# Encoder layer on one core: the mixer's tiles laid out anew, and more products read in four passes over 16-byte granules

## Chip, core and metric

One core of a Trainium2 chip runs one launch of the kernel. The metric is the device time of the launch in microseconds (us), the median over runs. The profile shown is one further execution, taken by the hardware profiler.

## What is computed

One layer of a hybrid encoder over 512 positions of width 1024, all in float32:

```
x = x + 1/2 * SwiGLU_1(RMSNorm(x))               # d_ff 2752
h = RMSNorm(x); u = h @ w_in                     # fourier 512 | q 8x64 | k 2x64 | v 2x64
A = Re(DFT2 over (positions, group channels)) per group of 128 channels, then a linear map per group
B = GQA attention: RMSNorm of q and k per head, 2-D rotary, bidirectional softmax
x = x + concat([A, B]) @ w_out
x = x + 1/2 * SwiGLU_2(RMSNorm(x))
y = RMSNorm_final(x)
```

## The kernel before

Everything lies transposed: channels on the 128 partitions, the 512 positions along a partition, so a tile `[128, 512]` of float32 takes 2048 bytes of each partition. Every operand of a large product is split into a high part, rounded to the type float32r, and a low part, the rest, and a product of two numbers is three matmuls: high x high, high x low, low x high. The function `product` issues these three. TensorE (PE) holds a 128 x 128 stationary operand, the weights, loads the next one while it streams the moving operand past the current one (up to 512 columns), and adds into one of 8 PSUM banks.

`product` has two branches. With `turn=True` (line 182) the moving operand and the output are read and written through `turned`:

```
def turned(ap):
    return ap.rearrange("p (a b c) -> p b a c", b=4, c=4)
```

The 512 columns are taken as 32 x 4 granules of 4 numbers (16 bytes): first granule 0 of each group of four, in a second pass granule 1, and so on. The same numbers are multiplied in another order; the output is permuted alike, so the result lies where it lay. The other branch (lines 184, 186, 187) reads the columns straight through. Before the change the first-layer products, the gate and down products and the projections of q, k and v are turned.

Three stages follow each other: the first SwiGLU (`ffn`, with Strassen-like products of 256 columns in line 418), the mixer, and the second `ffn` with the end. In the mixer the order of the work on every engine is written out by hand in the string `ORDER`, whose words name operations: `s` + query tile, head, block is a score product (lines 1147 and 1148, two matmuls: moving `kst`, the keys, weights a block of `qa` or `qb`), `m` the row maximum on VectorE (line 1153, tile `mx`), `e` the exponential on ScalarE (line 1161), `t` the transposition of the probabilities on PE (line 1173), `h` and `l` the high part on ScalarE and the low part on VectorE (tiles `ph`, `pl`; the subtraction is the helper in line 126), `v` the product with the values (line 1216, two matmuls: moving `ph` and `pl`, weights `vst`). This runs over 4 query tiles, 2 key heads and 4 blocks. `d` are the Fourier transform's position products (line 1070, tiles `pos` and `both`, weights `eh`, `el`), `c` its channel products, `f` its projections (lines 1011 to 1013). `y0` to `y7` are the output projection: 8 tiles of 8 blocks, each a straight `product` whose moving operands are `mh`, `ml` (that is `eh` and `el` again, reused for the Fourier results) and `qa`, `qb` (reused for the attention's result). Operands wait for each other by semaphores; each engine works its own list in order.

The second `ffn` ends in `closing`: the last three output tiles are computed for the first half of the positions in the usual layout, and for the other half by tokens (`by_tokens`, line 532): the tokens' activations are the weights, and the moving operand `tw`, lying in the ring of weight slots, has 384 columns. Its two blocks of 128 tokens need 7 x 3 matmuls each; between them row factors are computed (lines 247 to 267, 1394, 1395) and the results are scaled and written (lines 1355, 1404, 1409, 1419).

Where a tile lies in a partition follows from the pools, in the order in which tiles are allocated; `room` allocates a few unused bytes, `FRONT`, `LOWER`, `NEAR` and `FURTHER` shift operands within a larger tile. In the turned products moving operands begin 16 bytes past a multiple of 128 and weights 64 bytes past one; scores, values, `both` and the output products have both at 64.

Of the kernel before, what the change touches and what calls it, by code (L numbers as in the profile page):

```python
# [7 lines left out]
F32R = mybir.dt.float32r  # L8
# [17 lines left out]
FURTHER_IN = "f0", "f1", "f2", "f3"  # L26
ROOM = 64
FRONT, LOWER, NEAR = 16, -12, 4
NS = 12

GROUPS1 = ((0, "t", 1, 2), range(3, 9), range(9, 15), range(15, 21))
# [53 lines left out]
def encoder(ctx, tc, A, out):  # L85
# [8 lines left out]
    def room(pool, n):  # L94


        pool.tile([P, n // 4], F32, name=f"room{len(rooms)}")
        rooms.append(n)
# [76 lines left out]
    def turned(ap):  # L175
        return ap.rearrange("p (a b c) -> p b a c", b=4, c=4)
# [103 lines left out]
    def ffn(norm, after, wgu, wd, wdt, groups, opening, closing):  # L280
# [6 lines left out]
        with tc.tile_pool(name=f"act{n_}", bufs=1) as ap, tc.tile_pool(name=f"sums{n_}", bufs=2) as sp:  # L287
# [7 lines left out]
            def place(j):  # L295
# [3 lines left out]
            own, shared = slots[:KD], slots[KD:]  # L299

            tw = [
                ring[:, 3 * i * KD * P : 3 * i * KD * P + PLACES * LAST * P]
                .rearrange("p (m c) -> p m c", c=LAST * P) for i in range(2)
            ]

# [214 lines left out]
            def by_tokens(ps, c, group):  # L520

                t = slice(c * P, (c + 1) * P)
                for i in range(LAST):
                    nc.tensor.matmul(
                        ps[:, i * P : (i + 1) * P], x[KD - LAST + i][:, t], ident, is_transpose=True,
                        start=i == 0, stop=False, skip_group_check=True,
                    )
                for j in group:
                    h, l = (at[:, where[j], o, t] for o in range(2))
                    whi, wlo = (w[:, j - group[0]] for w in tw)  # L530
                    for a, b in ((h, whi), (l, whi), (h, wlo)):
                        nc.tensor.matmul(
                            ps[:, : LAST * P], a, b, start=False, stop=j == group[-1] and b is wlo, skip_group_check=True
                        )
                    yield

# [207 lines left out]
    n2 = Norm(2)  # L744
    with tc.tile_pool(name="mix", bufs=1) as mp, tc.tile_pool(name="mixt", bufs=1) as mt:

        room(mp, 192)
        more_tile = mp.tile([P, 2 * KD * P + ROOM], F32R, name="more")
        more = [slot_at(more_tile, i) for i in range(2)]
        plain.extend(more)  # L750
# [4 lines left out]
        cos = mp.tile([P, S], F32, name="cos")  # L755
        sin = mp.tile([P, S], F32, name="sin")
        chan = mp.tile([P, 4, P], F32R, name="chan")
        both = mp.tile([P, S], F32R, name="both")
        pos = mp.tile([P, 4 * 258 + 3 * 256], F32R, name="pos")
        room(mp, 32)  # L760

        coss = [[pos[:, (2 * p + i) * 258 : (2 * p + i + 1) * 258] for i in range(2)] for p in range(2)]
        sins = [[None, pos[:, 1032:1288]], [pos[:, 1288:1544], pos[:, 1544:1800]]]
        sc = mp.tile([P, 4, 10], F32, name="sc")
        room(mp, 32)


        ops = {}
# [136 lines left out]
        def query_ops(t):  # L905
            name = f"q{t}"
            rope_ops(name, qkg[:, 0:1])

            @op(f"{name}.ah")
            def _():  # L910
                qa[t] = mp.tile([P, S], F32R, name=f"qa{t}")
                nc.scalar.copy(qa[t][0:HD], rots[name][0:HD])

            @op(f"{name}.al")
            def _():
                lows(qa[t][HD:P], rots[name][0:HD], qa[t][0:HD])

            @op(f"{name}.bh")
            def _():
                qb[t] = mp.tile([P, S], F32R, name=f"qb{t}")  # L920
                nc.scalar.copy(qb[t][HD:P], rots[name][HD:P])

            @op(f"{name}.bl")
            def _():
                lows(qb[t][0:HD], rots[name][HD:P], qb[t][HD:P])

        kw = tp.tile([P, 4, 2, HD], F32, tag="wide", bufs=1, name="kw")
        kst = [[mp.tile([P, S], F32R, name=f"ks{v}{o}") for o in range(2)] for v in range(2)]

        def key_ops():  # L930

# [22 lines left out]
                op(f"k{v}.2")(lambda own=own, oth=oth, h2=h2: nc.scalar.copy(h2[oth], rots["k"][own]))  # L954
                op(f"k{v}.3")(lambda own=own, h1=h1, h2=h2: lows(h2[own], rots["k"][own], h1[own]))

        vst = mp.tile([P, 2, 4, 2, HD], F32R, name="vst")

        @op("vt")
        def _():  # L960
# [26 lines left out]

        eh, el = ([[mp.tile([P, 2, 256], F32R, name=f"e{n}{h}{i}") for i in range(2)] for h in range(2)] for n in "hl")  # L990

        for i in range(4):
            weight_ops(f"f{i}", A["winf"][i].rearrange("p a (b c) -> p (a b) c", c=P))
# [66 lines left out]
        def position_ops(g):  # L1060


            gs = slice(g % 2 * P, (g % 2 + 1) * P)
            dh, dl = hh[2 + g % 2], hl[2 + g % 2]
            name = f"d{g}"

            def add(w, m, t):
                ps, first = banks[name], not started
                started.append(t)
                nc.tensor.matmul(  # L1070
                    ps[:, t], w, m, start=first, stop=len(started) == 12, skip_group_check=True
                )

            started = []

            def sums(o):
                if not started:
                    banks[name] = bank_for(name, 1)
                for i in range(2):
                    h, l = (e[g // 2][i][:, o, gs] for e in (eh, el))  # L1080
                    t, m = (slice(256, 512), sins) if o else (slice(0, 258), coss)
                    if o and i == 0:
                        add(h, both, slice(0, S))
                        add(l, both, slice(0, S))
                    else:
                        add(h, m[0][i], t)
                        add(l, m[0][i], t)
                    add(h, m[1][i], t)

            op(f"{name}0")(lambda: sums(0))  # L1090
            op(f"{name}1")(lambda: sums(1))
            op(f"{name}.h")(lambda: nc.scalar.copy(dh, banks[name]))

            @op(f"{name}.l")
            def _():
                lows(dl, banks[name], dh)
                read(name)
# [41 lines left out]
        def score_ops(t, b, c):  # L1139
            n = f"{t}{b}{c}"  # L1140
            f = sc[:, c, 2 + 2 * t + b : 3 + 2 * t + b]

            @op(f"s{n}")
            def _():
                q = (qa, qb)[b][t][:, c * P : (c + 1) * P]
                sps[n] = bank_for(f"s{n}")
                nc.tensor.matmul(sps[n], q, kst[b][0], start=True, stop=False)  # L1147
                nc.tensor.matmul(sps[n], q, kst[b][1], start=False, stop=True)  # L1148

            @op(f"m{n}")  # L1150
            def _():
                mxs[n] = mx = tp.tile([P, 1], F32, tag="mx", bufs=8, name=f"mx{n}")
                nc.vector.tensor_reduce(out=mx, in_=sps[n], axis=AX.X, op=ALU.max, negate=True)
                nc.vector.tensor_tensor(out=mx, in0=mx, in1=f, op=ALU.mult)

            @op(f"e{n}")
            def _():
                if t not in zs:
                    zs[t] = tp.tile([P, 4, 2], F32, tag="z", bufs=2, name=f"z{t}")
                prob[t, b, c] = temp(f"e{n}")  # L1160
                nc.scalar.activation(
                    prob[t, b, c], sps[n], AF.Exp, bias=mxs[n], scale=f, accum_out=zs[t][:, c, b : b + 1]
                )
                read(f"s{n}")
# [42 lines left out]
        def attended_ops(t, b, kc):  # L1207
            n = f"{t}{b}{kc}"

            @op(f"v{n}")  # L1210
            def _():
                if kc == 0:
                    outs[t, b] = bank_for(f"o{t}{b}")
                w = vst[:, b, kc].rearrange("p a e -> p (a e)")
                for i, p in enumerate(parts[n]):
                    nc.tensor.matmul(outs[t, b], w, p, start=kc == 0 and i == 0, stop=kc == 3 and i == 1)  # L1216

            if kc < 3:
                return
            own = slice(b * HD, (b + 1) * HD)  # L1220

            @op(f"o{t}{b}.c")
            def _():
                if t not in pair:
                    pair[t] = tp.tile([P, S], F32, tag="u", name=f"oo{t}")
                nc.scalar.copy(pair[t][own], outs[t, b][HD:P])

            @op(f"o{t}{b}.a")
# [14 lines left out]
        def output_ops(d):  # L1243
            weight_ops(f"o{d}", A["wo"][d])
            name = f"y{d}"

            def step(k):
                if k == 0:
                    banks[name] = bank_for(name)
                whi, wlo = ws[f"o{d}"]  # L1250
                m = (mh[k], ml[k]) if k < 4 else (qa[k - 4], qb[k - 4])
                product(banks[name], whi[:, k, :], wlo[:, k, :], *m, k == 0, k == KD - 1)

            for k in range(KD):
# [309 lines left out]
```

## Time and profile before

| | us |
|---|---|
| median of 3 runs | 829.09 |
| lowest and highest | 829.08, 829.82 |
| profiled execution, whole | 829.21 |
| profiled execution, span from the first to the last instruction | 827.4 |

A row of a timeline gives the start, the duration, the engine (PE matmul, PEld weight load, DVE VectorE, ACT ScalarE, POOL GpSimd), the line, the operation, output<-inputs, and in brackets how long the engine was idle before and who released it. Rows of the same operation that follow each other are merged, with their count (x). A row of the chain of waits has start, duration, engine, output and line. A row of the windows has, for each engine, its busy time and its number of instructions, then the granted TensorE clock (1.00 is full speed) and the DMA engines' share.

### The profile page before, as it was taken

How to read it: one execution, taken by the hardware profiler on the slowest of the kernel's cores; microseconds unless marked ns; L12 is line 12 of the kernel's file. 1: busy time of each engine (PE TensorE's matmuls, PEld its weight loads, DVE VectorE, ACT ScalarE, POOL GpSimd, SP SyncE). 2: the span in 40 equal slices, each digit the busy share in tenths (PEclk: the TensorE clock that was granted, in tenths of full speed). 3: DMA queues.
4: the chain of work that ended last, by engine and by line, in shares of the span. 5: the costliest groups of instructions: out<-in, count | busy, mean ns of one | idle time of the engine just before them, and what ended most of it. 6: DMA issues, size and time to landing. Idle time of an engine off the chain costs nothing.

```text
span 827.4 us, 13668 instructions
## 1 busy us (share of the span) xinstructions
PE 820.0 (99%) x5406; PEld 750.9 (91%) x5406; DVE 639.4 (77%) x1005; ACT 464.6 (56%) x778; POOL 30.7 (4%) x34
## 2 busy tenths in 40 slices
PE   9999999999999999999999999999999999999997
PEld 7889999899989998888998888899988999899986
DVE  7998896489757847799998388998955896479573
ACT  7764663167424744778786357556632673256462
POOL 0110000000000000221000000100000000000001
PEclk9999999999999999999999999999999999999999
DMA  7664322323243213622020224443232332322222
GB/s 256 180 144 172 122 90 77 122 103 140 78 139 107 71 46 110 205 82 65 26 77 27 83 87 124 115 166 122 90 121 95 131 112 65 135 103 96 69 76 103
DMA packets 31169, 89.58 MB, mean 108 GB/s; under 512 B 3713, under 2 KB 8833, under 8 KB 31105
## 3 DMA queue, kind: packets, MB, share of 16 engines
q1 hardware_dynamic: 27776, 82.61, 29.4%
q0 software_dynamic: 2608, 5.12, 3.3%
q10 hardware_dynamic: 720, 0.98, 0.3%
q8 instruction: 42, 0.69, 0.3%
q14 instruction: 23, 0.18, 0.1%
HBM read 84.24 MB, written 2.10 MB: 104 GB/s over the span
## 4 chain that ended last, share of the span: by engine, by line
PE 97%; issue 1%; DVE 1%; DMA 0%; ACT 0%; POOLq 0%; POOL 0%; DVEq 0%
PE dn L182 25%; PE r L418 23%; PE q L418 12%; PE gu L182 8%; PE p L418 6%; PE mix L182 4%; PE gu L706 3%; PE mix L187 2%; PE mix L186 2%; PE mix L184 2%; PE mix L1216 2%; PE mix L1173 2%; PE mix L1147 1%; PE mix L1013 1%; PE mix L1148 1%; PE mix L1011 1%
## 5 line engine op out<-in xcount | busy, mean ns | idle before, releaser
L418 PE MATMUL r<-rt,ring 128*128 128x256 f32 x1686 | 209.3, 276 | 0.0
L182 PE MATMUL dn<-at,ring 128*128 128x512 f32 x900 | 203.3, 380 | 0.4 <-DVE ring L126 0.4
L418 PEld LDWEIGHTS r<-rt,ring 128*128 128x128 f32 x1686 | 200.4, 188 | 0.8
L182 PEld LDWEIGHTS dn<-at,ring 128*128 128x128 f32 x900 | 168.0, 188 | 29.8 <-DVE ring L126 1.6
L418 PE MATMUL q<-rt,ring 128*128 128x256 f32 x840 | 106.6, 276 | 0.0
L126 DVE TENSOR_TENSOR ring<-s,ring 128x1024 fp32r<-128x1024 f32 x70 | 85.5, 1221 | 23.9 <-ACT ring L377 20.8
L418 PEld LDWEIGHTS q<-rt,ring 128*128 128x128 f32 x840 | 100.4, 188 | 0.0
L541 DVE SCALAR_TENSOR_TENSOR gx<-dn,gx 128x512 f32<-128x512 f32 x61 | 41.9, 688 | 67.5 <-PE dn L182 67.5
L377 ACT CAST ring<-s 128x1024 fp32r<-128x1024 f32 x70 | 73.5, 1050 | 28.0 <-PE p L418 13.7
L168 ACT CAST ring<-raw_dn 128x768 fp32r<-128x768 f32 (+3 forms) x58 | 45.2, 783 | 71.4 <-PE dn L182 62.3
L126 DVE TENSOR_TENSOR ring<-raw_dn,ring 128x768 fp32r<-128x768 f32 (+3 forms) x58 | 51.6, 892 | 5.6 <-PE r L418 4.4
L418 PE MATMUL p<-rt,ring 128*128 128x256 f32 x420 | 53.3, 276 | 0.0
L126 DVE TENSOR_TENSOR ring<-raw_g,ring 128x1024 fp32r<-128x1024 f32 x35 | 42.7, 1221 | 11.2 <-PE p L418 10.2
L418 PEld LDWEIGHTS p<-rt,ring 128*128 128x128 f32 x420 | 50.2, 188 | 0.0
L182 PE MATMUL gu<-ring 128*128 128x512 f32 x216 | 48.9, 381 | 0.0
L182 PEld LDWEIGHTS gu<-ring 128*128 128x128 f32 x216 | 40.4, 188 | 6.9
L377 ACT CAST ring<-raw_g 128x1024 fp32r<-128x1024 f32 x35 | 36.8, 1052 | 16.1 <-DMA raw_g<-in_wgu 8.9
L426 ACT COPY p<-r 128x256 f32<-128x256 f32 x35 | 12.9, 370 | 46.4 <-PE r L418 46.1
L450 ACT ACTIVATE g<-g 128x512 f32<-128x512 f32 x35 | 22.2, 633 | 23.6 <-DVE g L449 23.3
L386 ACT CAST ring<-raw_u 128x512 fp32r<-128x512 f32 x35 | 21.8, 624 | 16.6 <-PE q L418 15.9
L254 POOL TENSOR_TENSOR r<-ms,mhalf 128x4 f32<-128x4 f32 (+1 forms) x4 | 4.3, 1071 | 660.9 <-DVE ms L247 660.9
L463 DVE TENSOR_TENSOR u<-g,u 128x512 f32<-128x512 f32 x35 | 24.1, 687 | 6.1 <-ACT u L462 6.0
(300 smaller groups left out, 1362.0 us busy)
## 6 DMA issues: line engine op xcount, KB each, us to landing
raw_g<-in_wgu SPq DMA_DIRECT2D x35, 512.0 KB, 3.6
raw_u<-in_wgu SPq DMA_DIRECT2D x35, 512.0 KB, 4.4
raw_dn<-in_wd SPq DMA_DIRECT2D x40, 384.0 KB, 3.1
raw_gu<-in_wgu SPq DMA_DIRECT2D x12, 512.0 KB, 3.5
raw_o<-in_wo SPq DMA_DIRECT2D x8, 512.0 KB, 3.5
raw_dn<-in_wd SPq DMA_DIRECT2D x8, 448.0 KB, 3.3
raw_wq<-in_wins SPq DMA_DIRECT2D x4, 512.0 KB, 4.3
raw_f<-in_winf SPq DMA_DIRECT2D x4, 512.0 KB, 4.2
```

Source lines behind the costliest of these rows:

```text
L126: nc.vector.tensor_tensor(out=lo, in0=src, in1=asf(hi), op=ALU.subtract)
L168: nc.scalar.copy(hi[:, :n, :], raw[:, :n, :])
L182: nc.tensor.matmul(ps, a, b, start=first and b is mhi and a is whi, stop=last and a is wlo)
L184: nc.tensor.matmul(ps, whi, mhi, start=first, stop=False)
L186: nc.tensor.matmul(ps[:, t], whi, mlo[:, t], start=False, stop=False)
L377: nc.scalar.copy(hi, src)
L386: nc.scalar.copy(hi, src)
L418: nc.tensor.matmul(ps[:, t], a[:, ks], b[:, i, t], start=first and i == 0 and o == 0, stop=i == KH - 1 and o == 2, skip_group_check=not first,
L450: nc.scalar.activation(b["g"], b["g"], AF.Silu)
L463: nc.vector.tensor_tensor(out=u, in0=b["g"], in1=u, op=ALU.mult)
L541: nc.vector.scalar_tensor_tensor(out=x[d][:, t], in0=ps[:, t], scalar=0.5, in1=x[d][:, t], op0=ALU.mult, op1=ALU.add)
L706: nc.tensor.matmul(turned(pss[c]), w[:, k % 2, c], turned(m[k]), start=k == 0 and m is hh and w is hi, stop=k == KD - 1 and w is lo,)
```

## The change

Four families of products go through `turned` as well: the scores, the values, the position products with `both`, and the eight output products (by `turn=True`). So do the last 384-column products, whose moving operand `tw` also begins 160 bytes (`ASIDE`, 40 numbers) further on. In the mixer the tiles are laid out in another order: the keys `kst`, `both` and `pos` come first; `qa`, `qb`, `eh`, `el` and `vst` become slices of one tile `near`, shifted by `NEAR` (4 numbers, 16 bytes); then follow `more`, `cos`, `sin` and `chan`. Moving operands of the output products then begin 16 bytes past a multiple of 128 against weights at 64; those of scores, values, `both` and the last products at 96 against weights at 16. The tiles of the temporary pool `mixt` all move by 96 bytes. The instructions, their number and their order on every engine stay; a few waits are attached to other instructions, among them the exp table load (line 1161), which gets the wait for the `mx` that the first exponential needs.

```
-                ring[:, 3 * i * KD * P : 3 * i * KD * P + PLACES * LAST * P]
+                ring[:, 3 * i * KD * P + ASIDE : 3 * i * KD * P + ASIDE + PLACES * LAST * P]
...
-                            ps[:, : LAST * P], a, b, start=False, stop=j == group[-1] and b is wlo, skip_group_check=True
+                            turned(ps[:, : LAST * P]), a, turned(b), start=False, stop=j == group[-1] and b is wlo,
+                            skip_group_check=True,
...
-        room(mp, 192)
+        room(mp, 96)
+        kst = [[mp.tile([P, S], F32R, name=f"ks{v}{o}") for o in range(2)] for v in range(2)]
+        both = mp.tile([P, S], F32R, name="both")
+        pos = mp.tile([P, 4 * 258 + 3 * 256], F32R, name="pos")
+        near = mp.tile([P, 18 * S + 2 * NEAR], F32R, name="near")
+        part = [near[:, NEAR + i * S : NEAR + (i + 1) * S] for i in range(16)]
+        eh, el = ([[part[4 * n + 2 * h + i]... for i in range(2)] for h in range(2)] for n in range(2))
+        vst = near[:, NEAR + 16 * S : NEAR + 18 * S].rearrange("p (v c o e) -> p v c o e", v=2, c=4, o=2)
+        room(mp, 32)
         more_tile = mp.tile([P, 2 * KD * P + ROOM], F32R, name="more")
...
-        both = mp.tile([P, S], F32R, name="both")
-        pos = mp.tile([P, 4 * 258 + 3 * 256], F32R, name="pos")
...
-                qa[t] = mp.tile([P, S], F32R, name=f"qa{t}")
+                qa[t] = part[8 + t]
...
-                qb[t] = mp.tile([P, S], F32R, name=f"qb{t}")
+                qb[t] = part[12 + t]
...
-                        add(h, both, slice(0, S))
-                        add(l, both, slice(0, S))
+                        add(h, turned(both), slice(0, S), turned)
+                        add(l, turned(both), slice(0, S), turned)
...
-                nc.tensor.matmul(sps[n], q, kst[b][0], start=True, stop=False)
-                nc.tensor.matmul(sps[n], q, kst[b][1], start=False, stop=True)
+                nc.tensor.matmul(turned(sps[n]), q, turned(kst[b][0]), start=True, stop=False)
+                nc.tensor.matmul(turned(sps[n]), q, turned(kst[b][1]), start=False, stop=True)
...
-                    nc.tensor.matmul(outs[t, b], w, p, start=kc == 0 and i == 0, stop=kc == 3 and i == 1)
+                    nc.tensor.matmul(turned(outs[t, b]), w, turned(p), start=kc == 0 and i == 0, stop=kc == 3 and i == 1)
...
-                product(banks[name], whi[:, k, :], wlo[:, k, :], *m, k == 0, k == KD - 1)
+                product(banks[name], whi[:, k, :], wlo[:, k, :], *m, k == 0, k == KD - 1, turn=True)
```

More of the change, by code (lines that the diff above doesn't have):

```diff
@@ L28 @@
 FRONT, LOWER, NEAR = 16, -12, 4
+ASIDE = 40
 NS = 12
@@ L745, in encoder @@
     with tc.tile_pool(name="mix", bufs=1) as mp, tc.tile_pool(name="mixt", bufs=1) as mt:
-        room(mp, 192)
+        room(mp, 96)
[4 more added lines that the diff above has]
+        part = [near[:, NEAR + i * S : NEAR + (i + 1) * S] for i in range(16)]
+        eh, el = ([[part[4 * n + 2 * h + i].rearrange("p (a b) -> p a b", a=2) for i in range(2)] for h in range(2)] for n in range(2))
+        vst = near[:, NEAR + 16 * S : NEAR + 18 * S].rearrange("p (v c o e) -> p v c o e", v=2, c=4, o=2)
+        room(mp, 32)
         more_tile = mp.tile([P, 2 * KD * P + ROOM], F32R, name="more")
@@ L757, in encoder @@
         chan = mp.tile([P, 4, P], F32R, name="chan")
-        both = mp.tile([P, S], F32R, name="both")
-        pos = mp.tile([P, 4 * 258 + 3 * 256], F32R, name="pos")
-        room(mp, 32)
         coss = [[pos[:, (2 * p + i) * 258 : (2 * p + i + 1) * 258] for i in range(2)] for p in range(2)]
@@ L764, in encoder @@
         sc = mp.tile([P, 4, 10], F32, name="sc")
-        room(mp, 32)
         ops = {}
@@ L927, in encoder @@
         kw = tp.tile([P, 4, 2, HD], F32, tag="wide", bufs=1, name="kw")
-        kst = [[mp.tile([P, S], F32R, name=f"ks{v}{o}") for o in range(2)] for v in range(2)]
         def key_ops():
@@ L955, in key_ops @@
                 op(f"k{v}.3")(lambda own=own, h1=h1, h2=h2: lows(h2[own], rots["k"][own], h1[own]))
-        vst = mp.tile([P, 2, 4, 2, HD], F32R, name="vst")
         @op("vt")
@@ L985, in encoder @@
             value_ops(v)
-        eh, el = ([[mp.tile([P, 2, 256], F32R, name=f"e{n}{h}{i}") for i in range(2)] for h in range(2)] for n in "hl")
         for i in range(4):
@@ L1065, in position_ops, with add @@
             name = f"d{g}"
-            def add(w, m, t):
+            def add(w, m, t, order=lambda ps: ps):
                 ps, first = banks[name], not started
@@ L1070, in add @@
                 nc.tensor.matmul(
-                    ps[:, t], w, m, start=first, stop=len(started) == 12, skip_group_check=True
+                    order(ps[:, t]), w, m, start=first, stop=len(started) == 12, skip_group_check=True
                 )
```

## The prediction

> **What bounds the kernel now.** I read the page first (busy shares, chain), then the windows by stage, then the timeline of PE around each group of products that the change touches, and last who waits for whom.
>
> ```profile
> span 827.4 us, 13668 instructions
> PE 820.0 (99%) x5406; PEld 750.9 (91%) x5406; DVE 639.4 (77%) x1005; ACT 464.6 (56%) x778; POOL 30.7 (4%) x34
> PE 97%; issue 1%; DVE 1%; DMA 0%; ACT 0%; POOLq 0%; POOL 0%; DVEq 0%
> ...
> core 0: us, PE busy (x) PEld busy (x) DVE busy (x) ACT busy (x) POOL busy (x), PEclk, DMA share, GB/s
> 356.00:449.00 93.00, 92.98 (x615) 83.61 (x614) 87.51 (x179) 71.29 (x145) 8.73 (x7) 1.00 0.17 52
> 449.00:492.00 43.00, 43.00 (x196) 35.72 (x195) 26.18 (x37) 17.49 (x26) 0.00 (x0) 1.00 0.23 74
> 809.00:828.00 19.00, 12.45 (x86) 11.80 (x85) 7.11 (x17) 4.00 (x10) 3.23 (x5) 0.90 0.31 111
> ```
>
> TensorE is the chain: 97% of it, busy in 820.0 of 827.4 us at the full clock (1.00). So the time is the number of matmuls times their spacing, and a product that is spaced closer shortens the span, unless PE then waits for somebody. Three stages hold what is changed. From 356 to 449 us run scores, softmax and values: VectorE is busy there 87.51 of 93.00 us, nearly as full as PE. From 449 to 492 run the output products y: VectorE 26.18 of 43.00, so it has room. From 809 on run the last 384-column products, where PE is busy 12.45 of 19.00. A row's mean duration (380 to 420 ns) is latency and overlaps its neighbours; the cost of a product is the distance between starts.
>
> **What one product costs in the two orders.** The trace has both orders side by side. Start times, first in the chain of waits, then in PE's timeline:
>
> ```profile
> 359.88 4.84 PE mix L182 x22
> ...
> 450.33 0.40 PE L184 MATMUL mix<-eh,ring 128*128 128x512 f32 x1
> ...
> 491.87 4.80 PE L182 MATMUL gu<-ring 128*128 128x512 f32 x21
> ...
> 356.06 0.40 PE L1147 MATMUL mix<-ks,qa 128*128 128x512 f32 x1
> ...
> 357.91 0.95 PE L883 MATMUL mix<-halves,sq_q 128*128 128x2 f32 x8
> ...
> 373.85 0.48 PE L1216 MATMUL mix<-ph,vst 128*128 128x512 f32 x1
> 374.17 0.40 PE L1216 MATMUL mix<-pl,vst 128*128 128x512 f32 x1
> ...
> 374.87 0.28 PE L1011 MATMUL mix<-ring 128*128 128x256 f32 x1
> ```
>
> L182 is the branch of `product` that already reads in 4 passes (`turned`): 4.84 us / 22 = 220 ns, and that in the crowded mixer. The output products (L184, L186, L187) read straight through: the first starts at 450.33, the gate products after them at 491.87, and 183 lie between (of 192, 8 tiles x 8 blocks x 3): 41.54 / 183 = 227 ns. Scores: 8 products from 356.06 to 357.91, 231 ns each. Values: 3 from 374.17 to 374.87, 233 ns. I take 232 for both. So a product turned like L182's saves 7 ns in y and 12 ns in scores and values. The first product behind a transposition takes 320 (373.85 to 374.17), some 88 more than the next; those 88 come with the change of operand kind, and I leave them as they are.
>
> Does the gain carry over? L182's moving operands begin 16 bytes past a multiple of 128, its weights 64 past one; scores, values and y start both at 64. The new layout puts y's at 16 and 64, exactly L182's pair. Scores, values, `both` and the last products get 96 and 16: another pair, the same distance between the two (80 modulo 128). For y the 220 is therefore seen; for the rest it is an inference. Their cost is bounded by 220 on one side and, since nothing excludes that the new place is worse, by the dearest spacing in the rows, 320, on the other; I take 220, which has the same distance and order.
>
> Against it stands a rule of the Trainium skill ("PSUM — Partial Sum Buffer", Specifications: PSUM lines are 8 bytes, and any non-contiguous access pattern slows matmuls significantly). The turned output is non-contiguous, so by that rule the sum would have the opposite sign. The trace disagrees: 220 ns turned against 227 straight.
>
> **The sum.** (1) y: 192 x 7 = 1.34 us, all on PE, with VectorE and ScalarE loosely filled behind it: counted in full.
>
> (2) Scores and values: 4 x 2 x 4 blocks of 2 products each, 128 x 12 = 1.54 us, and `both` 8 x 12 = 0.10. Here the cover is thin: the rows show that PE was already waiting for VectorE in this stage.
>
> ```profile
> 356.00:378.58 22.58, 4.12 (x10) 1.73 (x10) 1.00 0.27 72
> 378.58:391.20 12.62, 2.47 (x6) 1.12 (x6) 1.00 0.11 42
> ...
> 356.00:378.58 22.58, 1.81 (x6) 0.98 (x6) 1.00 0.27 72
> 378.58:391.20 12.62, 3.07 (x10) 1.65 (x10) 1.00 0.11 42
> ...
> 378.60 0.19 PEld L1147 LDWEIGHTS mix<-ks,qa 128*128 128x128 f32 x1 [0.21 <-DVE pl L126]
> ...
> 391.24 0.19 PEld L1147 LDWEIGHTS mix<-ks,qb 128*128 128x128 f32 x1 [0.26 <-ACT e L1161]
> ...
> 408.93 0.69 DVE L1153 TENSOR_REDUCE mx<-mix 128x1 f32<-128x512 f32 x1 [0.32 <-PE mix L1148]
> 414.40 0.69 DVE L1153 TENSOR_REDUCE mx<-mix 128x1 f32<-128x512 f32 x1 [0.64 <-PE mix L1148]
> ```
>
> The first two rows are L1147 in two windows, the next two L1216. The score at 378.60 waited for VectorE's `pl`; the one at 391.24 waited for ScalarE's `e`, which follows VectorE's `mx`. Where PE waits, what it won before is lost, unless VectorE comes earlier too, and VectorE's long waits on scores, 0.32 and 0.64 us, come at 408.93 and 414.40, behind those two points. Up to 391.2 there are 16 products of L1147, as many of L1148 and 16 of L1216: 48 x 12 = 0.58 us, which I count as lost. The other 80 x 12 = 0.96 and `both`, 0.10, I count in full: VectorE's idle time behind 391 is enough for it to follow. Part (2) gives 1.06 of 1.64.
>
> (3) The last products (L532):
>
> ```profile
> 811.56 1.82 PE L532 MATMUL last<-ring,at 128*128 128x384 f32 x9
> 813.22 0.72 PE L240 MATMUL ss<-ones,acc 128*128 128x2 f32 x6
> ...
> 816.29 1.88 DVE L1355 TENSOR_TENSOR gx<-gx,rp 128x512 f32<-128x512 f32 x3 [2.15 <-ACT rb L267]
> ...
> 818.09 0.15 DVE L1394 TENSOR_TENSOR squares<-squares,ms 128x1 f32<-128x1 f32 x1
> 818.33 0.55 POOL L1395 TENSOR_TENSOR r<-squares,mhalf 128x1 f32<-128x1 f32 x1 [0.56 <-DVE squares L1394]
> 818.93 0.32 PE L259 MATMUL rp<-ident,r 128*128 128x128 f32 x1
> ```
>
> Nine take 813.22 - 811.56 = 1.66 us; less one switch of 88 that is 175 ns each. Turned, 220 x 384/512 = 165 plus a little; estimate 167, 8 ns less. But only 27 of the 42 count: the 18 ahead of the row factor whose copy starts VectorE's L1355 (0.14 us), and the 9 after 818.93 (0.07). Those between end in PE's wait for POOL's `r`, which hangs on L1355 and is not moved by them. 0.21 us.
>
> (4) What moves without a product: all tiles of the mixer. Instructions and their order are the same on every engine; no DMA or queue moves. The 40 position products that stay straight (`pos`) get other distances to their weights; bounded by the 7 ns between the orders, 40 x 7 = 0.28 us either way, and taken as 0. The 128 transposes of the probabilities read `e`, which moves 96 bytes away from the identity:
>
> ```profile
> 365.19 0.88 PE mix L1173 x8
> ...
> 820.81 0.74 PE L1392 MATMUL xt<-ident,gx 128*128 128x128 f32 x5
> ```
>
> Today, at distance 0, they take 0.88 / 8 = 110 ns; L1392, whose operands lie 64 bytes apart, (0.74 - 0.28) / 4 = 115 without its last one's latency. So up to 5 ns x 128 = 0.6 us more or less; taken as 0, since the two hardly differ. The exp table load gets a wait that stood behind it:
>
> ```profile
> 357.45 1.28 ACT L1161 ACT_TABLE_LOAD   x1
> 359.36 0.78 ACT L1161 ACTIVATE e<-mix,mx,sc 128x512 f32<-128x512 f32 x1 [0.63 <-DVE mx L1154]
> ...
> 362.66 0.79 ACT L1161 ACTIVATE e<-mix,mx,sc 128x512 f32<-128x512 f32 x1
> 366.11 0.59 ACT L1178 CAST ph<-mix 128x512 fp32r<-128x512 f32 x1 [2.56 <-PE mix L1173]
> ...
> 365.03 1.04 PE L1173 MATMUL mix<-ident,e 128*128 128x128 f32 x8
> ```
>
> Before, the load ran at 357.45 while `mx` was still due; now it begins when `mx` is there, and the five exps queued behind it come 1.28 us later. The last is written at 363.45 (362.66 + 0.79); the transposes that read it start at 365.03, 1.58 later. That leaves 0.30 us, less what PE gains until then (12 products before 365, 0.14). ScalarE then idles 2.56 us before 366.11 and is level again. Cost 0; without that cover at most 1.28.
>
> Sum: 1.34 + 1.06 + 0.21 = 2.61 us. The profiled execution has 829.21 (827.4 of span and 1.8 around it); the median of three is 829.09. 829.09 - 2.61 = 826.5.
>
> **The rivals.** (A) Nothing is eaten: VectorE follows from the start and the 0.58 stays: 825.9. For it: part of VectorE's queue is itself released by PE. Against: the two waits quoted. (B) The mixer eats all of part (2), or the pair 96/16 brings nothing: 829.09 - 1.34 - 0.21 = 827.5. For it: VectorE's 87.51 of 93.00. Against: its waits on scores behind 400. (C) The change does not do what it says: 220 belongs to L182's surroundings, not to order and distance, and every product stays where it was: 829.1. Against: L182 has 220 in the mixer as in the gate. (D) Slower: at 96/16 the turned read restarts as a product behind a transposition does, 88 ns more for each of 136 products: +12.0 - 1.34 - 0.21, 839.5. It decides from 1.55 / 136 = 11 ns above today's spacing, 243 ns, and is slower beyond 0.2% from 256. The rule of the Trainium skill's "PSUM — Partial Sum Buffer" (Specifications) on non-contiguous patterns points this way. Against: the same order at the same distance costs 220.
>
> **How the numbers follow.** Forecast 0.60, A 0.17, B 0.11, C 0.06, D 0.06. 0.2% is 1.66 us, about what a measurement of this kernel can tell from no change: 827.4. Forecast and A are beyond it, and of B a part (its 827.5 lies at the border: 0.05 of 0.11): faster 0.82; C and the rest of B, 0.12, the same; D, 0.06, slower. The range: down to A less the 0.28 of `pos` and some of the transposes, 825.4; up to B and a little, 827.7. C and D lie outside.
>
> **What would show it.** Right: y's 183 products span 40.3 us instead of 41.54; scores and values in a row are 220 apart; new waits of PE for VectorE's `pl` and `mx` before 391 us, together about half a microsecond; POOL's `r` at the end makes PE wait longer. Wrong: y still at 227 (C); scores at 240 or more (D); no new waits in the mixer (A); PE in the mixer no earlier at 449 us although its products are closer (B); transposes at 365 waiting for `e` (the table load).

## The result

| | before | after |
|---|---|---|
| time, median, beside each other on one chip (8 runs each) | 829.42 us (829.08 to 829.93) | 827.11 us (826.84 to 827.66) |
| the profiled execution: time, span | 829.21, 827.4 us | 827.06, 824.8 us |

The ratio is 0.9973, with a 95% interval of 0.9962 to 0.9984: faster by 2.3 us, beyond the 0.2% that can be told from no change. The forecast was 826.5 us, its range 825.4 to 827.7.

The two spans differ by 2.6 us, the two times by 2.15. The last output transfer lands 0.4 us sooner behind the last matmuls in the profile after, but the part of the time that lies outside the span grew as much, from 1.8 to 2.26 us; why, no run tells. So the path is compared by PE's starts, not by the spans. First the profile's page of after (busy time and chain):

```profile
span 824.8 us, 13679 instructions
...
PE 816.9 (99%) x5406; PEld 750.4 (91%) x5406; DVE 639.2 (78%) x1005; ACT 464.6 (56%) x778; POOL 30.7 (4%) x34
...
PE 92%; DVE 5%; issue 1%; ACT 0%; DMA 0%; POOLq 0%; POOL 0%; DVEq 0%; ACTq 0%
```

PE's share of the chain fell from 97 to 92%, VectorE's rose from 1 to 5%. With closer products there are places now at which VectorE, not PE, sets the pace. Which stage, the windows of after tell (columns as before: PE, PEld, DVE, ACT and POOL busy, PE's clock, DMA share, GB/s):

```profile
356.00:449.00 93.00, 92.72 (x621) 84.20 (x620) 88.25 (x181) 71.88 (x146) 8.73 (x7) 1.00 0.16 52
449.00:492.00 43.00, 43.00 (x200) 36.75 (x199) 27.03 (x38) 18.95 (x28) 0.00 (x0) 1.00 0.21 74
```

In the mixer PE is idle for 0.28 us of 93 where it was idle for 0.02, with VectorE busy for 88.25. In the output products it is not idle at all. The products themselves, first y, in the chain of waits of after and in PE's timeline:

```profile
449.72 40.30 PE mix L183 x183
```

```profile
449.56 0.84 PE L183 MATMUL mix<-near,ring 128*128 128x512 f32 x3
...
489.87 0.82 PE L183 MATMUL gu<-ring 128*128 128x512 f32 x3
```

The y products run through the turned branch now (L183), and 183 of them take 40.30 us: 220 ns each. Their first start moved from 450.33 to 449.56 us, the first gate product behind them from 491.87 to 489.87. So 0.77 us was gained ahead of y and 1.23 in y. Scores and values, in PE's timeline of after:

```profile
356.11 0.40 PE L1150 MATMUL mix<-ks,near 128*128 128x512 f32 x1
356.35 0.38 PE L1151 MATMUL mix<-ks,near 128*128 128x512 f32 x1
...
357.67 0.39 PE L1151 MATMUL mix<-ks,near 128*128 128x512 f32 x1
...
373.80 0.47 PE L1219 MATMUL mix<-ph,near 128*128 128x512 f32 x1
374.11 0.38 PE L1219 MATMUL mix<-pl,near 128*128 128x512 f32 x1
...
374.77 0.28 PE L1014 MATMUL mix<-ring 128*128 128x256 f32 x1
```

From 356.35 to 357.67 lie six scores, 220 ns each, and from 374.11 to 374.77 three values, 220 each. The first product behind a transposition still takes 310 (373.80 to 374.11). Then the two places where PE waited before, the value product that stood at 385.02, and VectorE's two longest waits on scores (timeline of after):

```profile
378.62 0.19 PEld L1150 LDWEIGHTS mix<-ks,near 128*128 128x128 f32 x1 [0.38 <-DVE pl L127]
...
385.05 0.49 PE L1219 MATMUL mix<-ph,near 128*128 128x512 f32 x1
...
391.27 0.19 PEld L1150 LDWEIGHTS mix<-ks,near 128*128 128x128 f32 x1 [0.38 <-ACT e L1164]
...
408.69 0.69 DVE L1156 TENSOR_REDUCE mx<-mix 128x1 f32<-128x512 f32 x1 [0.20 <-PE mix L1151]
...
414.08 0.69 DVE L1156 TENSOR_REDUCE mx<-mix 128x1 f32<-128x512 f32 x1 [0.57 <-PE mix L1151]
```

Same places, same releasers, longer: 0.21 us became 0.38, and 0.26 became 0.38. And the starts did not move: 378.60 before and 378.62 after, 391.24 before and 391.27 after. From start to start of PE's matmuls the gaps are 413 and 414 ns, where they were 250 and 290, and a third, smaller one at 385.05 grew by 0.06 us: 0.35 in all. All that 48 products had won by then went into these waits. Behind 400 us VectorE's waits on scores became shorter, 0.32 to 0.20 and 0.64 to 0.57: there it does follow. Last, the end and the exp table load, in the timelines of after:

```profile
809.57 1.75 PE L533 MATMUL last<-ring,at 128*128 128x384 f32 x9
811.16 0.39 PE L241 MATMUL ss<-ones,acc 128*128 128x2 f32 x3
...
816.79 0.32 PE L260 MATMUL rp<-ident,r 128*128 128x128 f32 x1 [0.23 <-POOL r L1398]
818.46 0.28 PE L241 MATMUL ss<-ones,acc 128*128 128x2 f32 x2
...
359.44 1.28 ACT L1164 ACT_TABLE_LOAD   x1 [1.95 <-DVE sc L896]
...
364.03 0.80 ACT L1164 ACTIVATE e<-mix,mx,sc 128x512 f32<-128x512 f32 x1
...
365.02 1.04 PE L1176 MATMUL mix<-ident,e 128*128 128x128 f32 x8
```

Nine last products take 811.16 - 809.57 = 1.59 us instead of 1.66. PE's wait for POOL's `r`, which was below what the view marks, is 0.23 us. The table load did move behind `mx`, the fifth exp ends at 364.83, and the transposes start at 365.02 as they did (365.03): 0.19 us of cover was left.

### The profile page after: what moved, and what is told of

It is laid out like the page before. It is cut to its first block, busy times and chain, and to the rows that moved or that the text cites. A ratio compares the mean times of both kernels' runs of the same rounds, so it can differ in the third digit from the quotient of the medians.

```text
span 824.8 us, 13679 instructions
## 1 busy us (share of the span) xinstructions
PE 816.9 (99%) x5406; PEld 750.4 (91%) x5406; DVE 639.2 (78%) x1005; ACT 464.6 (56%) x778; POOL 30.7 (4%) x34
## 4 chain that ended last, share of the span: by engine, by line
PE 92%; DVE 5%; issue 1%; ACT 0%; DMA 0%; POOLq 0%; POOL 0%; DVEq 0%; ACTq 0%
PE dn L183 25%; PE r L419 23%; PE q L419 12%; PE gu L183 8%; PE mix L183 7%; PE p L419 6%; PE gu L708 3%; PE mix L1219 1%; PE mix L1176 1%; DVE mx L1156 1%; PE mix L1073 1%; DVE pl L127 1%; PE mix L1015 1%; PE mix L1016 1%; PE mix L1014 1%
## 5 line engine op out<-in xcount | busy, mean ns | idle before, releaser
L183 PE MATMUL dn<-at,ring 128*128 128x512 f32 x900 | 203.3, 381 | 0.5 <-DVE ring L127 0.4
L183 PEld LDWEIGHTS dn<-at,ring 128*128 128x128 f32 x900 | 168.0, 188 | 29.8 <-DVE ring L127 1.6
L183 PE MATMUL gu<-ring 128*128 128x512 f32 x216 | 48.9, 381 | 0.0
L183 PEld LDWEIGHTS gu<-ring 128*128 128x128 f32 x216 | 40.4, 188 | 6.9
```

Of the source, the lines that this page charges most:

```text
L183: nc.tensor.matmul(ps, a, b, start=first and b is mhi and a is whi, stop=last and a is wlo)
```

## The experiments

Each ran beside the kernel before, in four sets: it was at 829.9 us beside the four kernels that take order, layout and y apart, at 829.95 beside the lighter ones, the three products on GpSimd and the near tile 16 bytes back, at 829.2 beside the reordered ones and the near tile 16 bytes on, and at 830.07 beside the subtractions on GpSimd. Times are medians; the ratio and its interval are not those of the medians, but come from all runs of both kernels. **Two readings** carry most verdicts. y is the distance from the first of the 183 y products to the first gate product behind them. s/v is the mean start-to-start distance of those 56 score and value products that have a score or value product on both sides, so that no change of operand kind is in it. "Apart" is the distance of the moving operand's address to that of the weights, modulo 128 bytes, for y and for s/v.

| kernel | order | apart y, s/v | y, us | y, ns each | s/v, ns | time, us | ratio to before, 95% |
|---|---|---|---|---|---|---|---|
| before | straight | 0, 0 | 41.54 | 227.0 | 230.6 | 829.42 | |
| after | 4 passes | 80, 80 | 40.31 | 220.3 | 221.5 | 827.11 | 0.9973 [0.9962, 0.9984] |
| order alone | 4 passes | 0, 0 | 41.45 | 226.5 | 224.5 | 829.01 | 0.9989 [0.998, 0.9998] |
| layout alone | straight | 80, 80 | 42.10 | 230.0 | 232.9 | 830.38 | 1.0003 [0.9994, 1.0012] |
| y alone | y 4 passes | 80, 80 | 40.27 | 220.0 | 232.9 | 828.54 | 0.9982 [0.9973, 0.9991] |
| all but y | y straight | 80, 80 | 42.93 | 234.6 | 221.9 | 830.29 | 1.0005 [0.9996, 1.0014] |
| near tile 16 bytes back | 4 passes | 64, 96 | 42.38 | 231.6 | 226.2 | 829.90 | 0.9995 [0.9983, 1.0007] |
| near tile 16 bytes on | 4 passes | 96, 64 | 41.48 | 226.7 | 227.4 | 828.57 | 0.9992 [0.9983, 1.0001] |

### Order or distance

Theory 1: the 4-pass order and the distance of 80 bytes make the 220 ns together. Theory 2: the order does it alone. Theory 3: the distance alone. The first kernel has before's layout and turns all products.

```
-                product(banks[name], whi[:, k, :], wlo[:, k, :], *m, k == 0, k == KD - 1)
+                product(banks[name], whi[:, k, :], wlo[:, k, :], *m, k == 0, k == KD - 1, turn=True)
... (and turned(...) at scores, values, both and the last products; tiles where they were before)
```

> All products of the change read in four passes, but the tiles lie as before (moving operand and weights both 64 bytes past a multiple of 128, distance 0; the last products 64 against 16). Theory 1 (order and distance together make 220 ns): y products stay near 227 ns or above, scores and values near 232, the time within 0.7 us of before. Theory 2 (the order alone does it): y at 220, scores and values at 222, and the whole gain, 2.3 us.

The chain of waits of this kernel:

```profile
450.12 41.45 PE mix L182 x183
```

41.45 us: at distance 0 turning brings y 0.5 ns of its 6.7, and its spacings scatter from 218 to 240. Scores and values do gain, 6 of 9 ns. The time is 0.9 us below the kernel before; theory 2 falls for y and holds in part for scores and values.

The second kernel has the new layout and reads straight.

```
-                product(banks[name], whi[:, k, :], wlo[:, k, :], *m, k == 0, k == KD - 1, turn=True)
+                product(banks[name], whi[:, k, :], wlo[:, k, :], *m, k == 0, k == KD - 1)
... (and no turned(...) at scores, values, both and the last products; tiles as after)
```

> The new layout, every product of the change read straight through as before. Theory 1: y stays at 227 ns and scores and values at 232, the time within 0.5 us of before. Theory 3 (the distance of 80 bytes alone does it): y at 220, and most of the 2.3 us.

PE's timeline, the last y product and the first gate product:

```profile
492.67 0.39 PE L188 MATMUL mix<-near,ring 128*128 128x512 f32 x1
492.90 0.62 PE L183 MATMUL gu<-ring 128*128 128x512 f32 x2
```

230 ns: read straight, the new places are dearer than the old ones, by 3 ns in y and 2 in scores and values. Theory 3 falls. Neither half of the change brings the 220; both together do: theory 1.

### The parts by themselves

Both kernels have the layout of after. In one only y is turned, in the other all but y.

```
y alone:    turn=True for y;    sps, outs, add(h, both), last: straight
all but y:  y without turn=True; sps, outs, add(h, both), last: turned
```

> The new layout; of the changed products only the 192 output products read in four passes. Theory 1: y at 220 ns, 7 less than straight, 1.3 us gained, all of it kept, since VectorE has room there; scores and values stay at 232, the waits at 378.6 and 391.2 us stay at 0.21 and 0.26 us. Rival (the mixer's gain carries over into y, the two are not independent): less than 0.9 us.

```profile
450.88 40.27 PE mix L183 x183
```

The y products have their whole gain by themselves (the chain of waits shows 40.27 us), and the time is 1.36 us below the kernel before on that chip.

> As the changed kernel, but the 192 output products read straight through. Theory 1: scores and values at 222 ns, two waits of PE grown to about 0.35 and 0.4 us, 0.8 us left in the mixer and 0.2 at the end, 1.0 us in all; y at 227. Rival: nothing of the scores and values is kept, 0.2 us in all.

```profile
449.81 0.39 PE L185 MATMUL mix<-near,ring 128*128 128x512 f32 x1
...
492.75 0.82 PE L183 MATMUL gu<-ring 128*128 128x512 f32 x3
```

This one was a miss: 830.29 us, no gain that can be told. The mixer has its gain (from the first score to the first y product 93.50 us instead of 94.27), but the straight y products at their new place lose 42.93 - 41.54 = 1.39. They are at 235 ns here and at 230 in the kernel with the layout alone, with the same code for y and its operands at the same places; no run tells what makes the 5 ns.

### Is it 80, or any distance?

Near tile 16 bytes back:

```
-        part = [near[:, NEAR + i * S : NEAR + (i + 1) * S] for i in range(16)]
+        part = [near[:, 0 + i * S : 0 + (i + 1) * S] for i in range(16)]
... (vst likewise)
```

> The changed kernel with the tile of q, e and v shifted 16 bytes back: y's operands begin at 0 against weights at 64 (distance 64 instead of 80), those of scores and values at 96 against 0 (distance 96). Theory (the distance counts to 16 bytes): y leaves 220 ns, by 2 to 8 ns, and so do scores and values; up to 2 us slower than the changed kernel. Rival (any distance but 0 will do): y at 220, scores and values at 222, the same time.

```profile
450.43 42.38 PE mix L183 x183
```

Near tile 16 bytes on (`8 + i * S`; the expectation below misnames this shift as "32 bytes lower", the distances in it are right):

> The kernel after with the near tile's contents 32 bytes lower, so that operand and weights lie 96 bytes apart modulo 128 in the mixer's y products and 64 apart in scores and values (80 and 80 in the kernel after; 64 and 96 in the run before, which gave 231 and 226 ns). Theory of one good distance (80 alone gives 220): y leaves 220 for 225 or more, scores and values for about 231; +1.3 to +2.1 us in y and +0.7 to +1.1 in scores and values, time 829.2 to 830. Theory of a per-operand rule (the distance counts, but 96 is good for y too): y stays at 220 and only scores and values lose, 827.9.

```profile
449.83 41.48 PE mix L183 x183
```

16 bytes either way, and all of the gain in y is gone: 42.38 and 41.48 us, where 40.31 stood. By distance, over all kernels with the 4-pass order, y and s/v agree: 0 bytes 226.5 and 224.5, 64 bytes 231.6 and 227.4, 80 bytes 220.3 and 221.5, 96 bytes 226.7 and 226.2. The theory of one good distance holds among the four tried, and the rule by which 96 is good for y falls. One rival is left: between these kernels only the moving operand's place changes in y, and in scores and values, but for the kernel with the order alone, only the weights'; both families are closest where that operand begins 16 bytes past a multiple of 128. For the distance speaks that 64 apart is dearer than 96 in both, while by the operand's own place 0 is dearer than 32 in y (231.6 to 226.7) and cheaper in scores and values (226.2 to 227.4). No run separates the two for certain. The second kernel's time, 828.57, was below its 829.2 to 830, since s/v at 64 came out at 227 and not at 231.

The Trainium skill ("TensorE: Matmul & The Clock Gate", Step-by-step: what each phase is for) says that PE has two independent SBUF read ports, so that loading the next weights takes no read bandwidth from the running matmul. No run here shows whether the weight load is what costs time. But the two ports do not account for these runs: with the order fixed and nothing but the operand's place changed, a product takes from 220 to 231.6 ns.

### Is it VectorE that eats the mixer's part?

Kernels before and after, each without three of VectorE's products of 128x512 ahead of 391 us:

```
-                nc.vector.tensor_tensor(out=sw, in0=sw, in1=sin, op=ALU.mult)
+                if name not in SWAP_DMA:
+                    nc.vector.tensor_tensor(out=sw, in0=sw, in1=sin, op=ALU.mult)
```

> The kernel before, leaving out VectorE's product with the sines for q1, q2 and q3 (three instructions of 0.69 us, issued at about 346, 372 and 381 us). Theory (up to 391 us PE waits for VectorE, so products spaced closer win nothing there): the two waits of PE at 378.6 and 391.2 go, 0.3 us gained. Rival (PE's waits there come from ScalarE's own queue or from the scores themselves): no gain.

> The changed kernel, leaving out the same three instructions. Theory: the waits of 0.3 us each at 378.6 and 391.2 go, and the products ahead of them keep what they win: 0.6 us faster than the changed kernel, 2.9 us faster than the kernel before, and 2.6 us faster than the kernel before without the three. Rival: as the changed kernel, 2.3 us.

Times: 829.46 (ratio 0.9992 [0.9982, 1.0002]) and 827.24 (0.9964 [0.995, 0.9978]). Neither ratio differs from that of the full kernel by more than its interval, so the times cannot tell what lighter is worth; the traces can. Both profiled executions lost some 2.6 us at the very start, ahead of everything that was edited (the first score product begins at 358.69 and 358.67 us instead of 356.06 and 356.11), so distances from the first score product are compared:

| from the first score product to | before | after | before, lighter | after, lighter |
|---|---|---|---|---|
| the score that stood at 378.60 | 22.54 | 22.51 | 22.30 | 22.14 |
| the score that stood at 391.25 | 35.19 | 35.16 | 34.65 | 34.31 |
| the first y product | 94.27 | 93.45 | 93.74 | 92.53 |

PE's timeline of after, lighter, where the two waits stood:

```profile
380.81 0.47 PE L1151 MATMUL mix<-ks,near 128*128 128x512 f32 x1
...
392.98 0.49 PE L1151 MATMUL mix<-ks,near 128*128 128x512 f32 x1
...
531.07 1.05 ACT L378 CAST ring<-raw_g 128x1024 fp32r<-128x1024 f32 x1 [1.79 <-DMA raw_g<-in_wgu]
...
536.77 0.50 PE L183 MATMUL dn<-at,ring 128*128 128x512 f32 x1 [0.72 <-DVE ring L127]
```

The waits are gone. With VectorE as it is, the change brings 0.03 us by 391 us (35.19 to 35.16); with VectorE lighter, 0.34 (34.65 to 34.31). That is what 48 products at 9 ns less are worth, 0.43, but for a remainder. By the first y product it is 0.82 against 1.21. So VectorE's load is what eats that part: shown by where PE's products start, not by the times. Not all of this reaches the end. In after, lighter, PE waits 0.72 us for weights of the down projection, where after has this row:

```profile
534.84 0.49 PE L183 MATMUL dn<-at,ring 128*128 128x512 f32 x1 [0.44 <-DVE ring L127]
```

Some 0.28 us are given back there, behind a ScalarE cast that waited for a transfer of `raw_g` (531.07).

### Three tries at the lost part

**The three products on GpSimd:**

```
-                nc.vector.tensor_tensor(out=sw, in0=sw, in1=sin, op=ALU.mult)
+                (nc.gpsimd if name in SWAP_DMA else nc.vector).tensor_tensor(out=sw, in0=sw, in1=sin, op=ALU.mult)
```

> The changed kernel, with the same three products done by GpSimd, which is idle then and gets each operand by DMA some microseconds ahead of VectorE's turn (the whole result is computed). Theory: VectorE is relieved as in the kernel that leaves them out, less what GpSimd's slower pass (about 1.4 us for 512 columns, by its two passes over 256 in 1.43) makes VectorE's addition wait: 0.3 to 0.6 us faster than the changed kernel. Rival: VectorE and GpSimd hinder each other, or the additions wait, no gain or a loss of up to 1 us.

828.56 us, ratio 0.9979 [0.9969, 0.9988]: 1.4 us below the kernel before, where after is 2.3 below. The timeline:

```profile
371.65 1.52 POOL L877 TENSOR_TENSOR sw_q<-sw_q,sin 128x512 f32<-128x512 f32 x1 [8.91 <-DMA sw_q<-own_q]
372.06 1.66 DVE L127 TENSOR_TENSOR near<-rot_q,near 64x512 fp32r<-64x512 f32 x1
...
373.12 2.09 POOL L903 TENSOR_TENSOR sc<-sc,mhalf 128x8 f32<-128x8 f32 x1
373.74 0.69 DVE L878 TENSOR_TENSOR rot_q<-rot_q,sw_q 128x512 f32<-128x512 f32 x1
...
377.49 1.27 POOL L877 TENSOR_TENSOR sw_q<-sw_q,sin 128x512 f32<-128x512 f32 x1 [2.27 <-DMA sw_q<-own_q]
...
377.68 1.09 DVE L1157 TENSOR_TENSOR mx<-mx,sc 128x1 f32<-128x1 f32 x1
...
380.23 0.49 PE L1150 MATMUL mix<-ks,near 128*128 128x512 f32 x1 [1.32 <-DVE pl L127]
```

PE's small wait for `pl` became 1.32 us. VectorE was not relieved but held up: beside GpSimd's product from 377.49 to 378.76 its product of 128x1, which takes 0.16 elsewhere, took 1.09 and ended at 378.77; the subtraction of 64x512 at 372.06, 0.69 elsewhere, took 1.66 beside the product from 371.65. GpSimd's power of 128x8 (373.12) did no such thing: VectorE's sum at 373.74 took its usual 0.69 beside it, as far as GpSimd's recorded spans can be trusted.

**VectorE's list reordered**: the low halves that release PE at 378.62 ahead of a maximum, and the maximum and exp that release it at 391.27 ahead of low halves. The same on the kernel before.

```
-... q3.sd m102 h003 l003 t010 ...           +... q3.sd h003 l003 m102 t010 ...
-... h102 l100 s112 q3.s1 m111 e111 o01.a    +... h102 s112 q3.s1 m111 e111 l100 o01.a
```

> The kernel after with two changes of VectorE's order: the low halves l003 ahead of the score maximum m102 (the addition that PE's score product at 378.62 us waits for), and the maximum m111 with its exp e111 ahead of the low halves l100 (the exp that PE's score product at 391.27 us waits for). Nothing is left out. Theory L (what the mixer lost before 391 us is set by VectorE's place in its list, not by its load): both gaps of PE go, the spacings there fall from 413 and 414 ns to about 220, some 0.4 us, and the time is 826.7, ratio to the kernel before 0.9967. Rival M (VectorE's queue is full around there, so that the reordered words only delay others): new gaps of like size come behind 378 and 391 us, and the time stays 827.1. Rival R: the gain is given back at the down projection's first block near 535 us, where the run without the sine products lost 0.22 us to its weights: 826.9.

> The kernel before with the same two changes of VectorE's order. By theory L its smaller gaps at 378.6 and 391.2 us (spacings of 250 and 290 ns where 232 is usual) go: at most 0.1 us, 829.3 or no difference to be measured, so that with the result for the kernel after the reordering is worth 0.3 us more under the faster products than without them. By rival M no change or slower by up to 0.3 us.

827.06 us (0.9974 [0.9963, 0.9984]) and 829.21 (1.0001 [0.9992, 1.001]): nothing gained by either. PE's timeline of the reordered kernel:

```profile
378.53 0.47 PE L1150 MATMUL mix<-ks,near 128*128 128x512 f32 x1
...
385.26 0.50 PE L1219 MATMUL mix<-ph,near 128*128 128x512 f32 x1 [0.27 <-DVE pl L127]
...
391.15 0.66 PE L1176 MATMUL mix<-ident,e 128*128 128x128 f32 x4 [0.22 <-ACT e L1164]
391.56 0.47 PE L1150 MATMUL mix<-ks,near 128*128 128x512 f32 x1
```

The wait at 378 is gone (22.13 us from the first score, as in the lighter kernel), but waits of 0.27 and 0.22 us stand at 385.26 and 391.15, and at 391.56 the distance is 35.16 us, that of after to the digit. Rival M was right: VectorE's queue has no free place there, and an order only chooses who waits.

**Two of VectorE's subtractions of 128x1024 on GpSimd**, which is idle from 362 to 387 us in after:

```
-                lows(lo[:, :n, :], raws[name][:, :n, :], hi[:, :n, :])
+                lows(lo[:, :n, :], raws[name][:, :n, :], hi[:, :n, :], nc.gpsimd if name in LO_POOL else nc.vector)
+LO_POOL = ("f1", "f2")
```

> The kernel after with two subtractions of 128x1024 (the low halves of the first mixing weights f1 and f2, 1.22 us each on VectorE at 365.5 and 375.2 us) on GpSimd instead, where nothing ran from 362 to 387 us; every other word stays where it is, and nothing is left out. It is a theory against the reordered kernel: there VectorE's list stayed as full as before and its gain at 378 us came back as gaps at 385 and 390 us. Theory V (VectorE's load before 391 us sets PE's pace there): with 2.4 us less of it the gaps of PE at 378.62, 385.05 and 391.27 us go, as they did when the sine products were left out, for 0.5 to 0.8 us by 391.3 us; 0.2 of it may be given back at the down projection near 535 us, and the time is 826.4 to 826.7, below the kernel after. Rival G (GpSimd's subtractions are late or slow VectorE's own down): the low half of f2 ends after 379.2 us, where PE first reads it, or VectorE's operations beside it grow from 0.68 us; the time is 827.1 to 828.5.

830.03 us, ratio 0.9992 [0.9982, 1.0002]: no gain can be told any more, and the time lies above rival G's 827.1 to 828.5. The timeline and the windows (columns as above):

```profile
365.59 2.37 POOL L128 TENSOR_TENSOR ring<-raw_f,ring 128x1024 fp32r<-128x1024 f32 x1 [10.29 <-DVE ring L813]
365.99 1.98 DVE L1158 TENSOR_TENSOR mx<-mx,sc 128x1 f32<-128x1 f32 x1
...
373.98 2.45 POOL L128 TENSOR_TENSOR more<-raw_f,more 128x1024 fp32r<-128x1024 f32 x1 [4.42 <-ACT more L813]
374.10 2.88 DVE L870 TENSOR_TENSOR rot_q<-own_q,cos 128x512 f32<-128x512 f32 x1
...
378.79 0.76 PE L1177 MATMUL mix<-ident,e 128*128 128x128 f32 x5 [0.92 <-ACT e L1165]
380.11 0.54 PE L1151 MATMUL mix<-ks,near 128*128 128x512 f32 x1 [0.55 <-DVE pl L128]
```

```profile
380.00:381.00 1.00, 0.89 (x3) 0.76 (x4) 0.74 (x2) 1.00 (x3) 0.00 (x0) 0.72 0.14 57
381.00:382.00 1.00, 1.00 (x7) 1.00 (x6) 0.85 (x2) 0.25 (x2) 0.00 (x0) 0.50 0.00 0
382.00:383.00 1.00, 1.00 (x6) 1.00 (x6) 0.92 (x3) 0.87 (x2) 0.00 (x0) 0.50 0.00 0
```

A product of one number per partition took 1.98 us and ended at 367.97, where GpSimd's subtraction ended at 367.96. One of 128x512 took 2.88 us instead of 0.69. So in this execution the price was paid twice: VectorE stood still beside GpSimd, and PE's two waits, 1.47 us together, were followed by some 3.4 us at half the clock. The Trainium skill ("SBUF — State Buffer", Who interferes with whom) states the first: a VectorE instruction with two SBUF inputs contends with a GpSimd instruction that reads SBUF, for a port pair under an exclusive lock. These rows agree.

No version beat the kernel after.

## Why the prediction was right

- **Term 1, y: 1.34 us forecast for 192 products, 1.23 measured on the 183 that lie in one block.** They span 40.31 us where 40.3 was forecast. The inference held that y at L182's pair of places would have L182's 220.
- **Term 2, the spacing: 12 ns forecast, 9 measured** (230.6 to 221.5). The groups that were read for it gave 231 and 233, and 232 was taken; the mean over all such products was 230.6, and they came to 221.5, not 220. That the pair 96/16 brings what 16/64 does, because the distance is the same, was an inference, and the runs at three other distances bear it out. What the prediction did not say: the order without the distance would have given most of it for scores and values, and almost nothing for y.
- **Term 2, the part that is eaten: right in place and mechanism, mis-sized with the spacing.** All that was won ahead of 391 us was lost, 0.58 forecast, some 0.4 by 48 products at 9 ns: 0.29 of it at the two waits named and 0.06 at a third, at 385.05, that the prediction did not name. Behind 391 us the mixer kept 0.79 us (391.25 to 450.33 before, 391.27 to 449.56 after), not 1.06. That is 80 x 9 = 0.72 and a little for `both`.
- **Term 3, the end: 0.21 forecast, 0.22 measured.** PE's start before the first of the last products shows 1.99 us less (811.56 to 809.57), at the last `ss` 2.21 (820.67 to 818.46). What the products between had won went into the wait for POOL's `r`, as forecast.
- **Term 4, the moved places: 0 forecast, 0 seen.** The eight transposes at 365.02 take as long as before, and the table load stayed under its cover, with 0.19 us left where 0.30 less 0.14 was worked out.
- **The sum: 2.61 us forecast, 2.21 by PE's starts, 2.15 by the profiled executions, 2.31 by the medians.** Of the 0.4 that is missing 0.27 is term 2 and 0.11 term 1. The time itself was missed by 0.6 us, and half of that is not the sum's: the forecast counted from a median of 829.09, and beside the kernel after the kernel before came to 829.42.
- **The rivals.** A (nothing eaten): against it stand the two longer waits. B (the mixer brings nothing): 0.77 us by the first y product. C: every family is closer. D, the only slower one: no product restarts; 221.5 ns is far from the 243 at which it would decide. The rule on non-contiguous patterns that D leaned on ("PSUM — Partial Sum Buffer", Specifications, in the Trainium skill) is contradicted by every turned family of the kernel after: 220.3 against 227.0, 221.5 against 230.6.

## What to carry to other kernels

The spacing of these float32r products hung on the order of their reading and on where the operands lie, together, best told by the distance between moving operand and weights: copy the pair of places of a product that is already fast, distance and order both, since the order alone brought 0.9 us, the distance alone nothing, and a shift of 16 bytes took 1.2 to 2.1 us of y back. A gain per product counts only where PE does not wait for another engine a few microseconds later: read from the waits which products lie ahead of the last such wait, and take them out of the sum. Where that other engine is full, a new order of its list moves the wait, and products and subtractions moved from VectorE to GpSimd held up a VectorE operation with two operands in SBUF for as long as they ran.

## What the runs showed of the hardware that was not expected

- Read straight, a product at 80 bytes apart is dearer than at 0 (230.0 against 227.0 ns in y), while turned it is the cheapest. And the same straight y products took 230.0 ns in one kernel and 234.6 in another; this stays open.
- A VectorE product of one number per partition took 1.98 us beside a GpSimd subtraction of 2.37 us, where it takes 0.16 alone.
- PE's clock fell to 0.50 after waits of 0.92 and 0.55 us within 2.5 us (the profiled execution with the subtractions on GpSimd), and products of 256 columns went from 113 to 213 ns until 383.4 us. It did not come each time: the mean granted clock was 0.995 to 0.997 in six of the twelve executions of that kernel and 0.998 or more in the others. One wait of 1.32 us, in the profiled execution with the three products on GpSimd, left the clock at 1.00 (one of the twelve executions of that kernel had a mean of 0.995). The Trainium skill ("TensorE: Matmul & The Clock Gate", What's actually happening) puts the fall behind an idle window of about 3.4 us; here it came after less than half of that.
